# Sharing a PSUM tile between feature halves, and opening the second weight group early, at the joint between a transformer's output projection and its last MLP

## The chip, the core and the metric

The kernel runs on one core of a Trainium2 chip. TensorE (PE in the profile) multiplies matrices and writes into PSUM, VectorE (DVE) and ScalarE (ACT) do the elementwise work, GpSimd (POOL) does tiny per-row arithmetic here, and SyncE (SP) issues the DMA transfers. The metric is the time of one execution in microseconds (us), lower is better.

## The reference

The program is a two-layer backbone over 512 latent tokens and 256 context tokens of width 1024. Layer 0 mixes tokens by pooling, layer 1 by attention; each layer ends in an MLP of inner width 4096. Only the part around the end of layer 1 matters here:

```python
        y_lat, y_ctx = attention_mixer(h_lat, h_ctx, w_qkv[j], g_q[j], g_k[j], w_o[j], not last)
        x = x + gt1 * rms_norm(y_lat, g_mix_post[i])
        m_lat = sq_relu_mlp(modulate(rms_norm(x, g_mlp_pre[i]), sh2, sc2), w_mlp_in[i], w_mlp_out[i])
        x = x + gt2 * rms_norm(m_lat, g_mlp_post[i])

def sq_relu_mlp(h, w_in, w_out):
    return jnp.square(jax.nn.relu(h @ w_in)) @ w_out
```

In layer 1 only the 512 latent tokens go through the MLP. `attention_mixer` ends in a product with `w_o`, which this text calls the output stage.

## The kernel before

**Number format.** Each fp32 operand of a product is kept as two parts, hi and lo: ACT casts the value to the multiplier's format (hi) and DVE subtracts (lo = value - hi). One product is then three matmuls: hi with hi, hi with lo, lo with hi. "A product" below is one such matmul.

**The output stage** (`output`, lines 1334 to 1354). The 512 tokens are four tiles t = 0 to 3 of 128 rows. `attn_mm` (matmul line 1292) multiplies by the two column halves of `w_o`; `attn_ev` multiplies the result by the gate (DVE, line 326) and sums its squares (ACT, line 170); `rstd` turns the sum into a scale on POOL (lines 177 to 185). `norm_r` adds to the residual `xr` (DVE, line 329), `norm_s` sums the squares of the new `xr` (ACT line 170, then POOL), and `norm_c` scales the row (line 521 on ACT or 523 on DVE). When two tiles are ready, `norm_pair` calls `modulated_pair`: 16 TensorE transposes (line 350) turn the pair so that features lie on the partitions, DVE and ACT apply scale and shift (lines 358 and 361), and the result is written as hi (`h1H`, in `ra`) and lo (`h1L`, in `rb`). There are eight blocks k of 128 features. For the first pair (t = 0, 1) hi and lo are written four blocks at a time (lines 369 and 370), for the second pair (t = 2, 3) two at a time (lines 364 and 365, `fine`).

**The second MLP** (`mlp1`, from line 860). The inner width is cut in 16 groups of 256 features. A group's first half (`Inner.part`, matmul line 562) multiplies the tokens by 256 columns of `w_mlp_in`, as two feature halves f = 0 and 1 of 128 features each, over eight blocks k and three matmuls per block: 24 products for each f and each stretch of tokens. `relu` (line 573) and a square (line 902) on ACT follow. Groups go in pairs: the second half, with `w_mlp_out`, is done for two groups together by seven products of sums (`product`, matmul line 911) on operands X and W that `put` and `both` make on ACT and DVE (lines 883 and 889). A tile for a first half comes from the PSUM pool `psA`, which has two tiles of two banks. In group 0 each f has its own tile, and the tokens are cut in two chunks of 256, one in each bank: chunk 0 is the first pair, chunk 1 the second. Group 1 and all later ones do all 512 tokens in one matmul.

**What sets the order.** The steps of the output stage are put into a list with due times (`at(time, function, ...)`), which is sorted and traced. The framework then plans the order of each engine's instructions by its own model of time and puts in the waits; an instruction marked as kept in program order stays behind the one traced before it on its engine. In the first pass of `mlp1` (p = 0) the preparation of W is kept in this way. Weights arrive by a DMA into one of three `raw` buffers and are split into hi and lo (`split`, lines 142 and 145). The weights of group 0 are loaded and split within the output stage (due times 20 and 32); those of group 1 are loaded and split by `w_in(1, 1, ins[1], True)` at the start of `mlp1`, into `ra[:, 0:4096]`, which up to then holds the attention's output. Chunk 0 of group 0 is due at 41 and 42, the second pair at 47.4.

Of the kernel before, what the change touches and what calls it, by code (L numbers as in the profile page):

```python
# [68 lines left out]
def backbone(ctx: ExitStack, tc, x, ctx_in, w_ada, w_pool, pool_scale, w_qkv, g_q, g_k, w_o, w_mlp_in,  # L69
# [265 lines left out]
    def modulated_pair(t, i, s, hi, lo, works, wide, fine, on_act):  # L335
        place = lambda z, ks: z[:, ks, slice(t * P, (t + 2) * P)]
        ci = 0 if t < NL else 1
        sh = (SH1, SH2)[s] * KT
        pss = []
        for q in range(4):  # L340
            if not wide:
                ps = psB.tile([P, 2, 256], F32, tag="b", name="psx")
            elif q % 2 == 0:
                both = psA.tile([P, 4, 256], F32, tag="a", name="psx")
            if wide:
                ps = both[:, 2 * (q % 2):2 * (q % 2) + 2, :]
            for kk in range(2):
                k = 2 * q + kk
                for u in range(2):
                    te.transpose(ps[:, kk, u * P:(u + 1) * P], works[u][:, k * P:(k + 1) * P], ident)  # L350
            pss.append(ps)
        for q in range(4):
            h = works[q // 2][:, 512 * (q % 2):512 * (q % 2) + 512].rearrange("p (k n) -> p k n", n=256)
            for kk in range(2):
                k = 2 * q + kk
                sa, b = avec[i][s][:, k, ci:ci + 1], mods[i][:, sh + k, ci:ci + 1]
                if not on_act[k]:
                    ve.tensor_scalar(out=h[:, kk, :], in0=pss[q][:, kk, :], scalar1=sa, scalar2=b,
                                     op0=ALU.mult, op1=ALU.add)
                else:  # L360
                    sc.activation(h[:, kk, :], pss[q][:, kk, :], AF.Identity, scale=sa, bias=b)
            if fine:
                ks = slice(2 * q, 2 * q + 2)
                sc.copy(place(hi, ks), h)  # L364
                ve.tensor_tensor(out=place(lo, ks), in0=h, in1=place(hi, ks), op=ALU.subtract)  # L365
            elif q % 2:
                ks = slice(2 * q - 2, 2 * q + 2)
                h = works[q // 2].rearrange("p (k n) -> p k n", n=256)
                sc.copy(place(hi, ks), h)
                ve.tensor_tensor(out=place(lo, ks), in0=h, in1=place(hi, ks), op=ALU.subtract)  # L370

# [150 lines left out]
        else:  # L522
            ve.tensor_scalar(out=accv[:, t, :], in0=xr[:, t, :], scalar1=r, scalar2=None, op0=ALU.mult)

    def norm_pair(t, i, s, hi, lo, wide, fine, on_act):
        modulated_pair(t, i, s, hi, lo, [accv[:, t, :], accv[:, t + 1, :]], wide, fine, on_act)

    def chunks0(g):
        if g == 0:
# [1 line left out]
        return [[(0, 0, 0, 384), (1, 0, 384, 384)]], [(0, 2, 384, 0)]  # L531

    def chunks1(g):
        if g == 0:
            return [[(0, 0, 0, 256)], [(1, 0, 256, 256)]], [(0, 2, 256, 0)]
        return [[(0, 0, 0, 512)]], [(0, 1, 512, 0)]

    CHUNKS = {TOK: chunks0, LAT: chunks1}
    hids0 = [(rb[:, 3072 * b:3072 * b + 1536], rb[:, 3072 * b + 1536:3072 * b + 3072]) for b in range(2)]
    class Inner:  # L540
        def __init__(self, g, w, aH, aL, hid, chunks_of, ntok):
            self.w, self.a, self.ntok = w, (aH, aL), ntok
            self.hid = hid and [z.rearrange("p (f n) -> p f n", n=ntok) for z in hid]
            self.chunks, self.pieces = chunks_of(g)
            self.ps, self.opened = {}, set()

        def part(self, c, f, ks=range(KT)):
            (wH, wL), (aH, aL) = self.w, self.a
            if f not in self.ps:
                self.ps[f] = psA.tile([P, 2, 512], F32, tag="a", name="psin")  # L550
            ps, fs = self.ps[f], slice(f * P, (f + 1) * P)
            for k in ks:
                for n, (w, a) in enumerate(((wH, aH), (wH, aL), (wL, aH))):
                    for bank, o, t0, ln in self.chunks[c]:
# [7 lines left out]
                        te.matmul(ps[:, bank, o:o + ln], w[:, k, fs], rhs, start=start,  # L562
                                  stop=(k == KT - 1 and n == 2), skip_group_check=len(ks) < KT)

        def relu(self, f):
            r = work_tile()[:, 0:self.ntok]
# [149 lines left out]
    def w_in(i, g, rg, pin=False, wait=None):  # L716
        return rg.load(w_mlp_in[i, g], 256, pin, wait)
# [139 lines left out]
        before_last()  # L857
        finish(0, [part, (NG - 1, inner.hid, wo_)], order, last)

    def mlp1(inner, last):  # L860
        nonlocal xr, gate, junk
        for t in range(NL):
            sy.dma_start(spill[:, t], xr[:, t])
# [34 lines left out]

        def squares(inner, q):
            for f in range(2):  # L900
                inner.part(len(inner.chunks) - 1, f)
                sc.activation(F[:, q, f, :], inner.relu(f), AF.Square)
            return F[:, q, :, 0:256], F[:, q, :, 256:512]

# [397 lines left out]
        if ch:  # L1302
            rs[t] = rstd(ss1[t], 1 + len(ps1[t]))

    first1 = []

    def attention(st, base, unit_t):
        at = lambda i, fn, *args: st.at(base + unit_t * i, fn, *args)
# [23 lines left out]
        at(39.281, gate_diag if False else gate_rows, 1, GT1, 0)  # L1332

    def output(st, base):
        at = lambda i, fn, *args: st.at(base + i, fn, *args)
        for n, (ch, t) in enumerate(((0, 0), (0, 1), (1, 0), (0, 2), (1, 1), (0, 3), (1, 2), (1, 3))):
            b = 5.2 * n
            at(b, attn_mm, ch, t)
            at([5.2, 10.4, 15.6, 20.8, 26, 31.2, 36.4, 41.6][n], attn_ev, ch, t)
            if ch:  # L1340
                at([16.9, 27.3, 37.7, 42.9][t], norm_r, t, (False, False, False, False)[t])
                at([17.9, 28.3, 38.7, 43.9][t], norm_s, t, (False, False, False, False)[t])
                at([18.814, 29.214, 39.614, 46.4][t], norm_c, t, (False, True, True, False)[t])
                if t % 2:
                    at(36.3 if t == 1 else 47.4, norm_pair, t - 1, 1, 1, h1H, h1L, t == 1, t == 3,
                       ((False, True, True, False, True, False, True, False), (True, False, True, False, True, False, True, False))[t // 2])
# [22 lines left out]
    mlp1(first1[0], last1)  # L1369


_INS = ["x", "ctx", "w_ada", "w_pool", "pool_scale", "w_qkv", "g_q", "g_k", "w_o", "w_mlp_in", "w_mlp_out"]
# [79 lines left out]
```

## Time and profile before

| | us |
|---|---|
| median of three runs | 1178.41 (1176.73 to 1180.56) |
| the profiled execution | 1178.11 |
| its span, first to last instruction | 1176.3 |
| PE busy | 1145.3 (97%) |
| DVE busy | 938.4 (80%) |
| ACT busy | 635.0 (54%) |

All times of the trace below count from the start of the span. The output stage's matmuls run from 784.7 to 830.7; group 0's first product starts at 830.43 and group 1's last at 860.21. A row of the timeline gives the start, the length, the engine, the line, the operation, its output and inputs with shapes, and how many instructions are merged in it; in square brackets stand the idle time before it and what ended that. A row of the windows gives, after the stretch and its length, each engine's busy time and number of instructions, then the granted TensorE clock (1.00 is full), the share of the DMA engines and GB/s. Matmuls overlap, so the pace of a run of them is read from their starts.

### The profile page before, as it was taken

To read this page: it belongs to the slowest core of one execution; us is meant where nothing else is said; L and a number is where in the kernel's file an instruction comes from. 1 tells how busy PE (TensorE), PEld (TensorE's weight loads), DVE (VectorE), ACT (ScalarE), POOL (GpSimd) and SP (SyncE) were. 2 spreads that over 40 slices of the span, in tenths; PEclk is the share of its full clock that TensorE was granted. 3 is DMA by queue.
4 is the path that set the end of the run, shared out by engine and by line. 5 is a ranking of instruction groups with operands and counts; after the bars stand their busy time and mean duration, and the time that the engine had idled before them with its cause. 6 is when DMAs were issued, how large, how long until landed. Compare 5 with 4: busy or idle time off the path is not lost. (4 is left out here: it accounts for less than half of the span.)

```text
span 1176.3 us, 15958 instructions
## 1 busy us (share of the span) xinstructions
PE 1145.3 (97%) x6172; PEld 989.6 (84%) x6172; DVE 938.4 (80%) x1538; ACT 635.0 (54%) x1080; POOL 68.1 (6%) x120
## 2 busy tenths in 40 slices
PE   7889999999999999999999999999899999999997
PEld 5569898899899988998887889988888888888886
DVE  4677788889988998997778599877687779778876
ACT  4576655454454435555585378862676346435522
POOL 2030000000000000000231200001100000000001
PEclk9999999999999999999999999999999999999999
DMA  9983113343433434343422101115234123304212
GB/s 369 392 319 115 50 60 143 116 157 126 143 143 143 143 122 150 115 146 112 179 72 104 41 1 37 37 72 189 98 116 170 49 95 143 108 36 144 108 35 109
DMA packets 25516, 147.32 MB, mean 125 GB/s; under 512 B 2785, under 2 KB 5217, under 8 KB 9698
## 3 DMA queue, kind: packets, MB, share of 16 engines
q1 hardware_dynamic: 25442, 146.32, 34.1%
q8 instruction: 48, 0.79, 0.3%
q14 instruction: 26, 0.21, 0.1%
HBM read 138.96 MB, written 7.34 MB: 124 GB/s over the span
## 5 line engine op out<-in xcount | busy, mean ns | idle before, releaser
L807 PE MATMUL pso<-units,rb 128*128 128x512 f32 x1152 | 278.4, 392 | 0.0
L807 PEld LDWEIGHTS pso<-units,rb 128*128 128x128 f32 x1152 | 214.8, 188 | 41.2
L273 DVE SCALAR_TENSOR_TENSOR rows<-raw,cond,rows 128x256 f32<-128x256 f32 x280 | 127.0, 478 | 2.0
L819 DVE TENSOR_TENSOR acc<-acc,pso 128x512 f32<-128x512 f32 x129 | 85.4, 676 | 42.2 <-PE pso L807 42.1
L562 PE MATMUL psin<-ra,rb 128*128 128x512 f32 (+1 forms) x432 | 104.0, 343 | 1.6 <-ACT ra L364 1.6
L911 PE MATMUL pso<-units,pairs 128*128 128x512 f32 x336 | 82.3, 389 | 0.0
L562 PE MATMUL psin<-ra 128*128 128x512 f32 x256 | 80.6, 390 | 0.0
L562 PEld LDWEIGHTS psin<-ra,rb 128*128 128x128 f32 x432 | 70.9, 193 | 11.0 <-ACT ra L364 1.9
L911 PEld LDWEIGHTS pso<-units,pairs 128*128 128x128 f32 x336 | 63.1, 188 | 13.1
L915 DVE TENSOR_TENSOR acc<-acc,pso 128x512 f32<-128x512 f32 x72 | 48.7, 682 | 28.5 <-PE pso L911 28.5
L183 POOL TENSOR_SCALAR ms<-ss 128x1 f32<-128x1 f32 x20 | 11.2, 561 | 1006.7 <-ACT junk L170 963.8
L686 PE MATMUL psin<-ra,units 128*128 128x384 f32 x336 | 65.7, 337 | 0.4 <-ACT psin L698 0.4
L686 PE MATMUL psin<-sums,units 128*128 128x384 f32 x336 | 63.9, 337 | 0.0
L686 PEld LDWEIGHTS psin<-ra,units 128*128 128x128 f32 x336 | 59.7, 188 | 3.9 <-ACT psin L698 0.9
L686 PEld LDWEIGHTS psin<-sums,units 128*128 128x128 f32 x336 | 58.9, 188 | 1.7
L145 DVE TENSOR_TENSOR units<-raw,units 128x1024 fp32r<-128x1024 f32 (+2 forms) x49 | 55.3, 1150 | 3.6 <-ACT units L142 3.5
L562 PEld LDWEIGHTS psin<-ra 128*128 128x128 f32 x256 | 48.1, 188 | 10.0
L142 ACT CAST units<-raw 128x1024 fp32r<-128x1024 f32 (+2 forms) x49 | 46.8, 995 | 14.5 <-PE pso L807 10.4
L562 PE MATMUL psin<-rb 128*128 128x512 f32 (+1 forms) x144 | 53.4, 372 | 0.2 <-DVE rb L365 0.2
L817 ACT COPY acc<-pso 128x512 f32<-128x512 f32 x48 | 27.1, 587 | 49.0 <-PE pso L807 48.5
L1054 PE MATMUL psq<-units,ra 128*128 128x512 f32 x216 | 51.6, 392 | 0.0
L562 PE MATMUL psin<-rb,ra 128*128 128x512 f32 x128 | 49.8, 389 | 0.0
(277 smaller groups left out, 2347.2 us busy)
## 6 DMA issues: line engine op xcount, KB each, us to landing
raw<-in_w_ada SPq DMA_DIRECT2D x48, 1024.0 KB, 5.0
raw<-in_w_mlp_in SPq DMA_DIRECT2D x32, 1024.0 KB, 4.9
raw<-in_w_mlp_out SPq DMA_DIRECT2D x32, 1024.0 KB, 5.4
raw<-in_w_qkv SPq DMA_DIRECT2D x6, 1024.0 KB, 4.8
spill<-xr SPq DMA_DIRECT2D x10, 512.0 KB, 6.8
xr<-spill SPq DMA_DIRECT2D x10, 512.0 KB, 6.9
raw<-in_w_o SPq DMA_DIRECT2D x4, 1024.0 KB, 4.8
xr<-in_x SPq DMA_DIRECT2D x4, 512.0 KB, 6.3
```

What stands on the lines that cost most here:

```text
L142: a = sc.copy(hi, raw)
L145: b = ve.tensor_tensor(out=lo, in0=raw, in1=hi, op=ALU.subtract)
L183: gp.tensor_scalar(out=ms[:, 0:1], in0=ss[:, parts - 1:parts], scalar1=rest, scalar2=EPS, op0=ALU.add, op1=ALU.add)
L273: ve.scalar_tensor_tensor(out=r, in0=raw[:, k, :], scalar=cond[:, k, c:c + 1], in1=r, op0=ALU.mult, op1=ALU.add)
L562: te.matmul(ps[:, bank, o:o + ln], w[:, k, fs], rhs, start=start, stop=(k == KT - 1 and n == 2), skip_group_check=len(ks) < KT)
L686: te.matmul(bank, w[k], a[k], start=start and k == 0 and m == 0, stop=stop and k == 3 and m == 2, skip_group_check=True)
L807: te.matmul(pss[h][:, 0:cols[h][1]], a[:, f, ts_], w[:, f, cols[h][0]:sum(cols[h])], start=(n == 0 and not seeded[t]), stop=(n == len(seq) ...
L817: sc.copy(d, ps)
L819: ve.tensor_tensor(out=d, in0=d, in1=ps[:, 0:w], op=ALU.add)
L911: te.matmul(ps, a, w, start=(m == 0), stop=(m == len(seq) - 1))
L915: ve.tensor_tensor(out=M[n][:, t], in0=M[n][:, t], in1=ps, op=ALU.add)
L1054: te.matmul(ps, a[:, k, sl], w[:, k % 4, :], start=(k == 0 and n == 0), stop=(k == KT - 1 and n == 2))
```

## The change

Five things are changed, and nothing in the mathematics.

1. The first pair's second half of hi and lo (blocks 4 to 7) is no longer written where `modulated_pair` would do it. It is handed out (`late`) and written by a step `upper_half`, due at 41.65; its ACT copy is kept behind what was traced before it, which is the sum of squares of the last tile of the output stage.
2. Groups 0 and 1 become `paired`: both feature halves of a group use one `psA` tile, f = 0 in bank 0 and f = 1 in bank 1, and the two token chunks are the two halves of a bank.
3. Group 1 is also cut in two chunks of 256 tokens (four sets of 24 products of 256 columns in place of two sets of 24 of 512).
4. Group 1's weights are loaded at due time 26, and those of f = 0 are split in the output stage (`half_early`, due at 36) into `rb[:, 4096:6144]`. The other half is split at the start of `mlp1`.
5. Group 0's chunk 0 is traced as f = 0 and f = 1 over blocks 0 to 3, then over blocks 4 to 7. Between these come 12 products of group 1 (f = 0, chunk 0, blocks 0 to 3, due at 41.9); its other 12 (blocks 4 to 7) are due at 47.5, just after the second pair's transposes. `squares` then leaves out what has been done.

```diff
@@ modulated_pair
             elif q % 2:
                 ks = slice(2 * q - 2, 2 * q + 2)
                 h = works[q // 2].rearrange("p (k n) -> p k n", n=256)
+                if late is not None and q == 3:
+                    late.append((place(hi, ks), place(lo, ks), h))
+                    continue
                 sc.copy(place(hi, ks), h)
                 ve.tensor_tensor(out=place(lo, ks), in0=h, in1=place(hi, ks), op=ALU.subtract)
@@ chunks1
-        if g == 0:
-            return [[(0, 0, 0, 256)], [(1, 0, 256, 256)]], [(0, 2, 256, 0)]
+        if g < 2:
+            return [[(0, 0, 0, 256)], [(0, 256, 256, 256)]], [(0, 1, 512, 0)]
         return [[(0, 0, 0, 512)]], [(0, 1, 512, 0)]
@@ class Inner
-            if f not in self.ps:
+            if self.paired and not self.ps:
+                t = psA.tile([P, 2, 512], F32, tag="a", name="psin")
+                self.ps = {q: t[:, q:q + 1, :] for q in range(2)}
+            elif f not in self.ps:
                 self.ps[f] = psA.tile([P, 2, 512], F32, tag="a", name="psin")
+            if self.f0 and f == 0:
+                wH, wL = self.f0
...
+                            start = start and not (self.paired and (f, bank) in self.opened)
+                            self.opened.add((f, bank))
@@ mlp1
         def squares(inner, q):
             for f in range(2):
-                inner.part(len(inner.chunks) - 1, f)
+                for c in range(len(inner.chunks)):
+                    if (c, f) not in begun.get(inner, ()):
+                        inner.part(c, f)
                 sc.activation(F[:, q, f, :], inner.relu(f), AF.Square)
...
-        wi = [None, w_in(1, 1, ins[1], True)]
+        wi = [None, None]
+        hi, lo = (ra[:, z:z + 2048] for z in (0, 2048))
+        hi, lo = (z.rearrange("p (k n) -> p k n", n=256) for z in (hi, lo))
+        put((hi[:, :, P:], lo[:, :, P:]), raw1[0][:, :, P:], True)
+        second.w = hi, lo
+        begun = {inner: ((0, 0), (0, 1)), second: ((0, 0),)}
...
-            a12, a22 = squares(inner_of(2 * p + 1), 1)
+            a12, a22 = squares(inner_of(2 * p + 1) if p else second, 1)
@@ before attention and output
+    def half_early():
+        hi, lo = (rb[:, z:z + 1024].rearrange("p (k n) -> p k n", n=P) for z in (4096, 5120))
+        sc.copy(hi, raw1[0][:, :, 0:P])
+        ve.tensor_tensor(out=lo, in0=raw1[0][:, :, 0:P], in1=hi, op=ALU.subtract)
+        first1.append(Inner(1, (None, None), h1H, h1L, None, chunks1, LAT, True, (hi, lo)))
@@ output
+        def upper_half():
+            hi, lo, h = halves[0]
+            tc.keep_in_program_order(sc.copy(hi, h))
+            ve.tensor_tensor(out=lo, in0=h, in1=hi, op=ALU.subtract)
+
+        at(41.65, upper_half)
         for f in range(2):
-            at((41, 42)[f], lambda *a: first1[0].part(*a), 0, f)
+            for h in range(2):
+                at(41.7 + f / 10 + h, lambda *a: first1[0].part(*a), 0, f, range(4 * h, 4 * h + 4))
...
-        at(20, lambda: first1.append(Inner(0, w_in(1, 0, early, False, raws), h1H, h1L, None, chunks1, LAT)))
+        at(20, lambda: first1.append(Inner(0, w_in(1, 0, early, False, raws), h1H, h1L, None, chunks1, LAT, True)))
         at(32, lambda: split(*raws[0]))
+        at(26, lambda: raw1.append(raw_load(w_mlp_in[1, 1], rawp).rearrange("p (k n) -> p k n", n=256)))
+        at(36, half_early)
+        for h in range(2):
+            at((41.9, 47.5)[h], lambda ks: first1[1].part(0, 0, ks), range(4 * h, 4 * h + 4))
```

More of the change, by code (lines that the diff above doesn't have):

```diff
@@ L333, in scaled, with modulated_pair @@
         ve.tensor_scalar(out=dst, in0=xr[:, t, :], scalar1=r[:, 0:1], scalar2=None, op0=ALU.mult)
-    def modulated_pair(t, i, s, hi, lo, works, wide, fine, on_act):
+    def modulated_pair(t, i, s, hi, lo, works, wide, fine, on_act, late=None):
         place = lambda z, ks: z[:, ks, slice(t * P, (t + 2) * P)]
@@ L523, in norm_c, with norm_pair @@
             ve.tensor_scalar(out=accv[:, t, :], in0=xr[:, t, :], scalar1=r, scalar2=None, op0=ALU.mult)
-    def norm_pair(t, i, s, hi, lo, wide, fine, on_act):
-        modulated_pair(t, i, s, hi, lo, [accv[:, t, :], accv[:, t + 1, :]], wide, fine, on_act)
+    def norm_pair(t, i, s, hi, lo, wide, fine, on_act, late=None):
+        modulated_pair(t, i, s, hi, lo, [accv[:, t, :], accv[:, t + 1, :]], wide, fine, on_act, late)
     def chunks0(g):
@@ L540, in backbone, with __init__ @@
     class Inner:
-        def __init__(self, g, w, aH, aL, hid, chunks_of, ntok):
-            self.w, self.a, self.ntok = w, (aH, aL), ntok
+        def __init__(self, g, w, aH, aL, hid, chunks_of, ntok, paired=False, f0=None):
+            self.w, self.a, self.ntok, self.paired, self.f0 = w, (aH, aL), ntok, paired, f0
             self.hid = hid and [z.rearrange("p (f n) -> p f n", n=ntok) for z in hid]
@@ L561, in part @@
                             rhs = a[:, k, t0:t0 + ln]
+                            start = start and not (self.paired and (f, bank) in self.opened)
+                            self.opened.add((f, bank))
                         te.matmul(ps[:, bank, o:o + ln], w[:, k, fs], rhs, start=start,
-                                  stop=(k == KT - 1 and n == 2), skip_group_check=len(ks) < KT)
+                                  stop=(k == KT - 1 and n == 2), skip_group_check=len(ks) < KT or self.paired)
         def relu(self, f):
@@ L858, in mlp0, with mlp1 @@
         finish(0, [part, (NG - 1, inner.hid, wo_)], order, last)
-    def mlp1(inner, last):
+    def mlp1(inner, second, last):
         nonlocal xr, gate, junk
@@ L1334, in output @@
     def output(st, base):
[L1335 removed]
+        at, halves = lambda i, fn, *args: st.at(base + i, fn, *args), []
         for n, (ch, t) in enumerate(((0, 0), (0, 1), (1, 0), (0, 2), (1, 1), (0, 3), (1, 2), (1, 3))):
@@ L1368, in backbone @@
     mlp0(first[0], hids0, (4, 5, 0, 1, 2, 3), extra0, mid0, last0, before0)
-    mlp1(first1[0], last1)
+    mlp1(*first1, last1)
 _INS = ["x", "ctx", "w_ada", "w_pool", "pool_scale", "w_qkv", "g_q", "g_k", "w_o", "w_mlp_in", "w_mlp_out"]
```

4 lines of the change are left out of this document (2 added, 2 removed).

## The prediction

> **What bounds the kernel now.** I read the page first, then one window from the joint to almost the last matmul, then the joint itself.
>
> ```profile
> span 1176.3 us, 15958 instructions
> PE 1145.3 (97%) x6172; PEld 989.6 (84%) x6172; DVE 938.4 (80%) x1538; ACT 635.0 (54%) x1080; POOL 68.1 (6%) x120
> 848.00:1168.00 320.00, 320.00 (x1431) 265.14 (x1431) 252.22 (x296) 156.72 (x207) 2.66 (x6) 1.00 0.28 102
> ```
>
> From 848 to 1168 PE is busy in every microsecond at full clock. So whatever moves PE earlier at the joint moves the end by as much, unless a new wait takes it back. The joint, in four stretches: group 0's first token chunk, the gap, its second chunk, group 1.
>
> ```profile
> 830.43:836.65 6.22, 6.22 (x54) 6.18 (x52) 3.29 (x4) 3.06 (x6) 1.49 (x3) 1.00 0.09 33
> 836.65:841.57 4.92, 1.69 (x14) 1.29 (x13) 2.73 (x6) 2.58 (x6) 0.79 (x2) 1.00 0.18 70
> 841.57:849.40 7.83, 7.61 (x48) 7.35 (x48) 6.97 (x8) 4.87 (x7) 0.00 (x0) 0.78 0.11 33
> 849.40:860.43 11.03, 11.03 (x50) 9.12 (x49) 9.05 (x10) 7.80 (x10) 0.00 (x0) 1.00 0.39 144
> ...
> 843.60:846.80 3.20, 3.20 (x18) 3.20 (x16) 0.50 0.00 0
> ```
>
> PE loses time in two ways: it is idle in most of the 4.92 us of the gap, and right after it the clock is granted at 0.50 for 3.2 us. The idle pieces and their releasers, from the timeline of PE, with four rows for the pace:
>
> ```profile
> 836.53 0.28 PE L562 MATMUL psin<-ra,rb 128*128 128x256 f32 x1
> 838.41 1.53 PE L350 MATMUL psx<-ident,acc 128*128 128x128 f32 x12 [1.59 <-DVE acc L523]
> 841.57 0.50 PE L562 MATMUL psin<-ra,rb 128*128 128x256 f32 x2 [1.64 <-ACT ra L364]
> 842.30 0.39 PE L562 MATMUL psin<-rb 128*128 128x256 f32 x1 [0.23 <-DVE rb L365]
> ...
> 843.60 0.63 PE L562 MATMUL psin<-ra,rb 128*128 128x256 f32 x2
> 846.80 0.48 PE L562 MATMUL psin<-ra,rb 128*128 128x256 f32 x2
> 847.12 0.28 PE L562 MATMUL psin<-rb 128*128 128x256 f32 x1
> 849.27 0.28 PE L562 MATMUL psin<-ra,rb 128*128 128x256 f32 x1
> ```
>
> From 847.12 to 849.27 lie 18 products of 256 columns: 0.119 us each. Group 1's 48 of 512 columns take 11.03 us, 0.230 each. What sets the 838.41 is the chain of waits (start, length, what), with ACT's and DVE's own rows around its beginning:
>
> ```profile
> 831.26 0.61 issue
> 831.87 0.48 ACT junk L170 x2
> 832.52 0.89 POOL ms L183
> 833.48 0.56 POOL rs L185
> 834.04 2.61 issue
> 837.56 317.36 issue
> ...
> 830.80 0.41 DVE L326 TENSOR_TENSOR acc<-psy,gate 128x256 f32<-128x256 f32 x1
> 830.93 1.04 ACT L369 CAST ra<-acc 128x1024 fp32r<-128x1024 f32 x1
> 832.00 1.23 DVE L370 TENSOR_TENSOR rb<-acc,ra 128x1024 fp32r<-128x1024 f32 x1 [0.79 <-ACT ra L369]
> 834.07 1.28 DVE L329 SCALAR_TENSOR_TENSOR xr<-acc,rs,xr 128x1024 f32<-128x1024 f32 x1 [0.85 <-POOL rs L185]
> ```
>
> It is the last tile's normalization, queued behind the upper-half cast at 830.93. From 837.56 on the chain has only "issue": PE runs on.
>
> **The change part by part.**
>
> *Group 1's 24 products in the gap.* Twelve take 12 x 0.119 = 1.43 us. The first twelve follow group 0's blocks 0 to 3, the second stand behind the transposes, against idle pieces of 1.59 and 1.64 us: both fit and delay nothing. After the gap group 1 has 72 products of 256 columns: 72 x 0.119 = 8.57 us in place of 11.03. **Gain 2.46 us.** (All 96 would take 11.42: the narrower cut costs 0.4 us, in these figures.)
>
> *The clock.* From 843.60 to 846.80, the stretch at 0.50, 15 products take 3.20 us, 0.213 each; at 0.119 they would take 1.79. With both idle pieces down to some 0.2 us I expect no drop: **gain 1.4 us**. Bounds: 0, the drop stays; 1.5, a little beyond the 3.2 us.
>
> *The upper half written later.* The sum of squares at 831.87 comes up to 0.62 us earlier, as the 1.04 us cast no longer stands before it (DVE has read that tile at 830.80 + 0.41 = 831.2). The cast then ends near 832.8 and the subtraction (1.23) near 834.1. If DVE does it before the residual, as listed, the residual starts at 834.1, as now (834.07): 0. If the residual goes first, it can start at 832.9, since POOL's 0.89 also shrinks: up to 1.1 earlier, of which PE, now busy to 836.65 + 1.43 = 838.1, can use some 0.4. If both end late, 0.6 is lost. I take 0, the listed order. Group 0's blocks 4 to 7 need this subtraction: PE reaches them at 830.43 + 36 x 0.12 = 834.8, covered by the 12 products of group 1; without them PE would wait 0.8 us.
>
> *The early split and its load.* Rows for its cost and cover:
>
> ```profile
> 804.13 0.33 SPq L123 DMA_DIRECT2D raw<-in_w_mlp_in  x1
> 823.15 0.69 DVE L326 TENSOR_TENSOR acc<-psy,gate 128x512 f32<-128x512 f32 x1 [4.09 <-PE psy L1292]
> 823.94 0.60 ACT L170 ACTIVATE junk<-psy 128x512 bf16<-128x512 f32 x1 [3.36 <-DVE acc L326]
> 844.77 1.05 ACT L883 CAST ra<-raw 128x1024 fp32r<-128x1024 f32 x1
> 847.12 1.22 DVE L883 TENSOR_TENSOR ra<-raw,ra 128x1024 fp32r<-128x1024 f32 x1
> ```
>
> The one DMA is issued at 804.13 already now, so on SP's queue nothing is passed that matters, and the buffer is held until after the joint as before: 0. The half split costs ACT 1.05 and DVE 1.22 us; ACT idles 3.36 and DVE 4.09 us right where it is due: 0. If that cover is missed, it stands before the first pair's work and PE starts late by up to 2.3 us, the other bound. The same work disappears behind the joint, where DVE is nearly full. POOL issues nothing new.
>
> *Later stages.* PE comes 3.9 us sooner, DVE and ACT only 2 to 3. One idle piece of DVE, and the two closest meetings:
>
> ```profile
> 851.20 0.69 DVE L889 TENSOR_TENSOR work<-hid 128x512 f32<-128x512 f32 x1 [1.72 <-ACT hid L902]
> 870.61 0.68 DVE L883 TENSOR_TENSOR pairs<-hid,pairs 128x512 fp32r<-128x512 f32 x1
> 874.03 1.98 PE L911 MATMUL pso<-units,pairs 128*128 128x512 f32 x8
> 877.72 2.29 DVE L145 TENSOR_TENSOR ra<-raw,ra 128x2048 fp32r<-128x2048 f32 x1 [2.29 <-ACT ra L142]
> 882.19 0.39 PE L562 MATMUL psin<-ra 128*128 128x512 f32 x1
> ```
>
> The third product's operand is ready 2.7 us before its use, group 3's weights 2.2 us. With DVE ahead by half a split (1.07) and by the idle time it now spends waiting for group 0 (1.7), both hold by about 1 us. I take 0; at worst 2 us come back.
>
> **Sum:** 2.46 + 1.4 + 0 = 3.9 us. The profiled execution took 1178.1 us, 0.3 below the median; 1178.1 - 3.9 = 1174.2.
>
> **The rivals.**
>
> *Clock stays halved* (idle near 838 and the transposes are enough): gain 2.5, 1175.6. For it: the drop came 2 us after PE had resumed, so it looks back over several microseconds. Against: the gap loses 2.9 of 3.2 idle us.
>
> *The gain is taken back* by the late operands above: 2 us, 1176.2.
>
> *The shared tile makes TensorE wait for ScalarE: slower.* Today each f has its own tile. If waits are kept by whole PSUM tile, the matmuls of f = 1 must wait until `relu` of f = 0 has read. Rows that bear on this:
>
> ```profile
> 553.53 2.35 PE L686 MATMUL psin<-ra,units 128*128 128x384 f32 x12 [0.43 <-ACT psin L698]
> 59.65 3.13 PE L490 MATMUL pspool<-rb,ra 128*128 128x256 f32 x24
> 62.90 0.60 ACT L170 ACTIVATE junk<-pspool 128x512 bf16<-128x512 f32 x1 [2.32 <-PE pspool L490]
> 862.48 0.61 ACT L573 ACTIVATE work<-psin 128x512 f32<-128x512 f32 x1
> ```
>
> At 553.53 product 3 of layer 0's MLP writes bank 1 of a tile and waits for a copy that touches only bank 0 of it; at 62.90 ACT, idle, reads a first bank only when the 24 matmuls of both are done. So such waits are likely. They are harmless while ACT is prompt: group 1's f = 0 covers the `relu` of group 0, and group 0's f = 1 (24 x 0.119 = 2.9 us) that of group 1. But now ACT reads group 1's f = 0 at 862.48, when its products ended near 849.40 + 24 x 0.230 = 854.9: 7.6 us late, its queue standing behind the W chain. Were it as late now, PE would idle 7.6 + 0.6 - 2.9 = 5.3 us and lose 1.4 to the clock: -3.9 + 6.7 = +2.8, or 1180.9; with a second such wait for group 0, beyond 1182. It decides from 6.8 us of lateness on. Against it: the planner knows the wait and can put that `relu` first, and before 849 ACT is not behind.
>
> [...] The row at 553.53 shows a wait across banks, so here the measurement decides for the wait.
>
> **How the numbers follow.** A measurement of this kernel can tell about 0.3%, 3.5 us, from no change. Against the profiled 1178.1 that bound lies at 1174.6. Forecast, 1174.2, its own range 1172.8 to 1175.1 (the chain's bounds of 0.4 earlier and 0.6 later, the clock's, and a short wait in the later stages): 0.62, of which 0.08 falls above 1174.6. Clock or late operands, 1175.6 to 1176.2: 0.16. Shared-tile wait, 1178 to 1184: 0.22, nearly all of it beyond 0.3%, since such a stall brings its own clock drop and may come twice; 0.03 within. So faster 0.54, same 0.08 + 0.16 + 0.03 = 0.27, slower 0.19. The range runs from 1172.3 to 1180.5 and leaves out the worse half of the last rival.
>
> **What would show it.** Right: 24 products of line 562 with 256 columns in the gap, twelve on each side of the transposes; idle pieces below 0.5 us; granted clock 1.00 from 840 to 850; group 1 done near 856.4; 320 us later no PE idle. Wrong: PE idle released by ACT line 573 between 845 and 865 (shared tile), PE idle released by line 883 or 145 between 868 and 880 (late operands), a clock of 0.50 after the gap, or the first pair's hi and lo later than 830.4.

## The result and the profile after

The changed kernel is slower. Its median is 1188.39 us (five runs, 1184.1 to 1190.34) against 1178.41 (five runs): a ratio of 1.0074 (95% interval 1.0058 to 1.009). Timed once more in a later experiment it took 1184.32 against 1178.45: 1.0048 (1.003 to 1.0066). The forecast was 1174.2.

The profiled execution took 1188.43 us. The head of its page:

```profile
span 1186.6 us, 16056 instructions
PE 1151.7 (97%) x6220; PEld 995.5 (84%) x6220; DVE 938.1 (79%) x1539; ACT 635.4 (54%) x1081; POOL 67.0 (6%) x120
```

PE is busy 6.4 us longer with 48 more instructions, the second token chunk of group 1. The span is 10.3 us longer. To see where, I cut it at group 0's first product and at the last matmul row. The timeline of PE after, with all idle pieces of the joint (groups 0 and 1 are cut in chunks of 256 tokens, group 2 in one of 512, so a row of 512 columns is group 2's or a later one's; the rows of 851.07 and 852.27 have no idle time before them and are explained below):

```profile
833.85 0.28 PE L572 MATMUL psin<-ra,rb 128*128 128x256 f32 x1
842.95 1.47 PE L350 MATMUL psx<-ident,acc 128*128 128x128 f32 x12
846.06 0.50 PE L572 MATMUL psin<-ra,rb 128*128 128x256 f32 x2 [1.40 <-ACT ra L364]
846.79 0.39 PE L572 MATMUL psin<-rb 128*128 128x256 f32 x1 [0.23 <-DVE rb L365]
851.07 0.52 PE L572 MATMUL psin<-ra,rb 128*128 128x256 f32 x3
852.27 0.28 PE L572 MATMUL psin<-ra,rb 128*128 128x256 f32 x1
854.62 0.39 PE L572 MATMUL psin<-ra,rb 128*128 128x256 f32 x1 [2.06 <-ACT work L583]
861.61 0.50 PE L572 MATMUL psin<-ra,rb 128*128 128x512 f32 x1 [2.37 <-ACT work L583]
862.93 2.08 PE L923 MATMUL pso<-ra,pairs 128*128 128x512 f32 x4 [0.50 <-ACT pairs L893]
892.25 0.50 PE L572 MATMUL psin<-ra 128*128 128x512 f32 x1 [0.60 <-ACT ra L142]
1178.90 0.88 PE L817 MATMUL pso<-units 128*128 128x256 f32 x6
```

and the last row of the same timeline before:

```profile
1168.58 0.88 PE L807 MATMUL pso<-units 128*128 128x256 f32 x6
```

From the first product to that last row lie 345.05 us after (833.85 to 1178.90) and 338.15 before (830.43 to 1168.58). I call this length the stretch below. So 6.9 us come from the joint on and 3.4 us from ahead of it. Those 3.4 us are complete by 94 us, where the instructions of the two kernels and their order are the same; what they are stands in the last section.

The idle pieces tell the story. The piece of 1.59 us is gone, as forecast, and the one of 1.64 is 1.40. But two new ones are ended by ACT's line 583, the `relu` that reads the PSUM tile (line 573 before): 2.06 and 2.37 us. All pieces add up to 7.16 us after and 3.46 before. The two other new ones are short waits for late operands (0.50 at 862.93, 0.60 at 892.25). The windows of PE after, from the joint on:

```profile
833.85:842.95 9.10, 9.10 (x76) 8.95 (x75) 4.13 (x6) 3.35 (x6) 1.88 (x5) 1.00 0.15 59
855.30:858.70 3.40, 3.40 (x18) 3.40 (x17) 0.21 (x1) 0.00 (x0) 0.00 (x0) 0.50 0.00 0
861.90:865.40 3.50, 3.00 (x8) 2.02 (x8) 3.42 (x5) 1.56 (x3) 0.00 (x0) 0.53 0.22 54
900.00:1178.00 278.00, 278.00 (x1239) 230.10 (x1238) 220.93 (x264) 128.29 (x168) 2.67 (x6) 1.00 0.27 97
```

The clock is not halved behind the gap now (granted 1.00 from 843 to 855), but it is halved once behind each of the two waits for a `relu`; from 900 on PE is busy in every microsecond. ACT's own timeline shows why it was late, first after, then around the same place before:

```profile
852.08 1.04 ACT L893 CAST ra<-work 128x1024 fp32r<-128x1024 f32 x1 [2.61 <-DVE work L899]
853.03 1.04 ACT L893 CAST units<-raw 128x1024 fp32r<-128x1024 f32 x1
853.98 0.59 ACT L583 ACTIVATE work<-psin 128x512 f32<-128x512 f32 x1
859.16 1.90 ACT L142 CAST rb<-raw 128x2048 fp32r<-128x2048 f32 x1 [3.94 <-PE psin L572]
860.97 0.59 ACT L583 ACTIVATE work<-psin 128x512 f32<-128x512 f32 x1
868.93 0.60 ACT L583 ACTIVATE work<-psin 128x512 f32<-128x512 f32 x1
879.81 0.60 ACT L583 ACTIVATE work<-psin 128x512 f32<-128x512 f32 x1 [6.28 <-PE psin L572]
```

```profile
848.75 0.60 ACT L573 ACTIVATE work<-psin 128x512 f32<-128x512 f32 x1 [2.93 <-PE psin L562]
851.72 1.04 ACT L883 CAST ra<-work 128x1024 fp32r<-128x1024 f32 x1
```

*The first wait.* In the order that the framework planned for PE, 14 products of group 1's f = 0 stand among the 24 of group 0's f = 0. So the last of the 24 is one of the three at 851.07, and PE's signal to ACT stands in the trace at 851.37. ACT does not take the `relu` then. Two casts of the W chain come before it in ACT's order, and the first of them waits for DVE until 852.08 (ACT is idle for 2.61 us, 0.7 of it after 851.37). The `relu` runs at 853.98, 2.6 us late. PE has only 10 products of group 1 left to do meanwhile, up to 852.27, and then waits before f = 1 of group 0, which is in the same tile. In the kernel before, the `relu` (848.75) stands ahead of the same casts (851.72 is the first).

*The second wait* is at group 2's first product. The two `psA` tiles are handed out in turn, so group 2 gets group 0's, which is free only after the `relu` of f = 1 at 860.97. Before that `relu` ACT does the 1.90 us split of group 2's weights. The split goes into the place of group 0's weights, so it too can start only when PE is done with group 0 (the row of 859.16 ends an idle time of 3.94 with PE). PE has nothing else to do: group 1's f = 1 shares a tile with its f = 0, which ACT reads only at 868.93, and it stands behind group 2's f = 0 in PE's order.

### The profile page after: what moved, and what is told of

Same layout as the page of the kernel before. It is cut to its first block, busy times and chain, and to the rows that moved or that the text cites. A ratio compares the mean times of both kernels' runs of the same rounds, so it can differ in the third digit from the quotient of the medians.

```text
span 1186.6 us, 16056 instructions
## 1 busy us (share of the span) xinstructions
PE 1151.7 (97%) x6220; PEld 995.5 (84%) x6220; DVE 938.1 (79%) x1539; ACT 635.4 (54%) x1081; POOL 67.0 (6%) x120
## 5 line engine op out<-in xcount | busy, mean ns | idle before, releaser
L572 PE MATMUL psin<-ra,rb 128*128 128x256 f32 (+1 forms) x464 | 111.7, 342 | 5.8 <-ACT work L583 4.4
L572 PEld LDWEIGHTS psin<-ra,rb 128*128 128x128 f32 x464 | 77.0, 196 | 15.9 <-ACT work L583 5.1
L572 PE MATMUL psin<-ra 128*128 128x512 f32 (+1 forms) x256 | 76.4, 376 | 0.6 <-ACT ra L142 0.6
L572 PE MATMUL psin<-rb 128*128 128x512 f32 (+1 forms) x160 | 58.1, 364 | 0.2 <-DVE rb L365 0.2
L572 PE MATMUL psin<-rb,ra 128*128 128x512 f32 (+1 forms) x128 | 48.1, 376 | 0.0
```

## The experiments

The theory was: PE waits for the `relu`s because waits are kept by whole PSUM tile and ACT's order puts the `relu` late. The rivals: the tile alone is harmless and the early products, their place, or the late upper half cost the time; or the clock does. Since one profile can hold a halving of the clock and another of the same kernel not, each stretch stands with the number of halvings in it. "Medians" are this kernel's and that of the kernel before in the same comparison.

| kernel | medians, us | ratio (95%) | stretch | halvings in the joint |
|---|---|---|---|---|
| before | 1178.41 | | 338.15 | 1 |
| after | 1188.39 / 1178.41 | 1.0074 (1.0058 to 1.009) | 345.05 | 2 |
| after, again | 1184.32 / 1178.45 | 1.0048 (1.003 to 1.0066) | 344.42 | 2 |
| relu_last | 1178.91 / 1178.29 | 1.0008 (0.9996 to 1.0019) | 335.43 | 0 |
| relu_last, again | 1177.07 / 1178.45 | 0.9988 (0.9977 to 0.9999) | 336.82 | 1 |
| twelve_pinned | 1182.51 / 1178.29 | 1.0041 (1.0027 to 1.0056) | 339.15 | 1 |
| relu_last_pinned | 1175.68 / 1178.2 | 0.9977 (0.9964 to 0.9991) | 334.29 | 0 |
| shared_only | 1180.09 / 1178.29 | 1.0016 (1.0002 to 1.003) | 339.41 | 0 |
| shared_only_relu_last | 1179.09 / 1178.29 | 1.0006 (0.9993 to 1.002) | 337.29 | 0 |
| own_tiles | 1175.26 / 1178.2 | 0.9978 (0.9964 to 0.9992) | 333.83 | 0 |
| own_no_late | 1174.71 / 1178.45 | 0.9971 (0.9959 to 0.9982) | 334.14 | 0 |
| late_only | 1177.87 / 1178.2 | 0.9997 (0.9985 to 1.001) | 336.35 | 0 |
| before_tail | 1178.88 / 1178.2 | 1.0007 (0.9996 to 1.0018) | 336.65 | 0 |

**The `relu`s of a paired group moved behind the products of both halves** (relu_last).

```diff
             for f in range(2):
                 for c in range(len(inner.chunks)):
                     if (c, f) not in begun.get(inner, ()):
                         inner.part(c, f)
-                sc.activation(F[:, q, f, :], inner.relu(f), AF.Square)
+                if not inner.paired:
+                    sc.activation(F[:, q, f, :], inner.relu(f), AF.Square)
+            if inner.paired:
+                for f in range(2):
+                    sc.activation(F[:, q, f, :], inner.relu(f), AF.Square)
```

> The changed kernel, with one edit: in a paired group the ReLU and square of f = 0 and f = 1 both come after the products of both halves, so no product is behind a read of its tile; same tiles, same early products, same result. Theory A (the shared PSUM tile makes TensorE wait for ScalarE's ReLU): the idle pieces of 2.06 and 2.37 us released by that ReLU go, the second drop of the clock with them, and group 1 runs right behind group 0; from group 0's first product to group 1's last some 26.5 to 28 us where before took 30.0, so 1174.5 to 1177. Rival B (the early products ahead of the transposes, and ScalarE's and VectorE's queues as rearranged, are the loss, the ReLU wait only shows it): TensorE waits as long elsewhere, for W or X operands, and the time stays above 1183.

No PE row of the joint is ended by line 583 any more; what is left is the gap's 1.40 and 0.23. The stretch falls by 9.6 us against the changed kernel, some 2.9 of them, by an estimate, its two halvings (1.39 to 1.50 us each between kernels of the same joint, below). The ratio to the kernel before is 1.0008, so nearly the whole loss is given back, though the expected gain on the kernel before (1174.5 to 1177) did not come. ACT is no faster here:

```profile
857.34 1.90 ACT L142 CAST rb<-raw 128x2048 fp32r<-128x2048 f32 x1 [0.81 <-DMA raw<-in_w_mlp_in]
859.15 1.08 ACT L583 ACTIVATE work<-psin 128x512 f32<-128x512 f32 x2
```

Both `relu`s of group 0 still stand behind the casts and the split. But no product of group 0 is behind its own tile's read any more, and the rest of group 1's products lie between group 0's last product and group 2's first.

**The second twelve products kept behind the transposes** (twelve_pinned). In the changed kernel 70 of the 72 products of the gap stand ahead of the twelve transposes on PE, ten of them from the twelve that are due after.

```diff
+        def second_part(ks, pin):
+            ordered[0] = pin
+            first1[1].part(0, 0, ks)
+            ordered[0] = False
         for h in range(2):
-            at((41.9, 47.5)[h], lambda ks: first1[1].part(0, 0, ks), range(4 * h, 4 * h + 4))
+            at((41.9, 47.5)[h], second_part, range(4 * h, 4 * h + 4), h == 1)
```

> The changed kernel, with one edit: the second twelve early products of group 1 are kept in program order, behind the second pair's transposes, as their due time says; in the changed kernel 10 of these 12 stand ahead of 12 transposes. Theory A: the transposes come some 1.2 us sooner and the 1.40 us idle piece before group 0's second chunk is filled, but the ReLU waits are as long or longer, so little is won: 1185 to 1188. Rival B: the loss falls by more than half, below 1183.

The transposes and two idle pieces of this kernel's PE, then four rows of its ACT:

```profile
838.19 1.47 PE L350 MATMUL psx<-ident,acc 128*128 128x128 f32 x12
841.30 0.50 PE L572 MATMUL psin<-ra,rb 128*128 128x256 f32 x2 [0.21 <-ACT ra L364]
853.15 0.50 PE L572 MATMUL psin<-ra,rb 128*128 128x512 f32 x1 [2.37 <-ACT work L583]
...
847.00 0.60 ACT L583 ACTIVATE work<-psin 128x512 f32<-128x512 f32 x1 [2.30 <-PE psin L572]
848.16 1.03 ACT L893 CAST ra<-work 128x1024 fp32r<-128x1024 f32 x1
850.70 1.90 ACT L142 CAST rb<-raw 128x2048 fp32r<-128x2048 f32 x1 [0.55 <-PE psin L572]
852.50 0.59 ACT L583 ACTIVATE work<-psin 128x512 f32<-128x512 f32 x1
```

The transposes start 8.01 us after the first product (830.18), where the changed kernel has 9.10, and the piece behind them falls from 1.40 to 0.21. The first wait for the `relu` is gone, which was not expected: the planner now has that `relu` (847.00) ahead of the W cast (848.16), and ACT reads as soon as PE is done. The tile is shared as before, and PE has only 7 products of group 1 to do meanwhile; so it is ACT's order that made the first wait long. The wait of 2.37 for group 0's tile is untouched: the split (850.70) still stands before the `relu` of f = 1 (852.50). The time, 1182.51, is just below the 1183 that was set for the rival; theory A's 1185 to 1188 counted on both waits. The kernel stays slower than the one before. Its profiled execution (1178.87) was well below its median, so the ratio is what counts here.

**Both edits together** (relu_last_pinned; the two diffs above).

> The changed kernel with both edits: both ReLUs of a paired group behind both halves, and the second twelve early products kept behind the second pair's transposes. From group 0's first product to the start of the last matmul, before took 338.2 us and the run with the ReLU edit alone 335.4. If the two faults (ReLU wait, twelve products ahead of the transposes) are separate, the 1.40 us piece goes to about 0.2 and this stretch is 334.0 to 334.8, with no wait for the ReLU. Rival: the planner or a late operand takes it back, and the stretch stays at 335.4 or more. The whole time less than before by 2 to 4 us only if the part ahead of the joint is as in before; if the clock's drops at the start are again more than in before, the whole gains nothing.

The ends of the stretch, the transposes and all idle pieces of the joint:

```profile
830.44 0.28 PE L572 MATMUL psin<-ra,rb 128*128 128x256 f32 x1
838.45 1.47 PE L350 MATMUL psx<-ident,acc 128*128 128x128 f32 x12
841.56 0.50 PE L572 MATMUL psin<-ra,rb 128*128 128x256 f32 x2 [0.21 <-ACT ra L364]
842.29 0.38 PE L572 MATMUL psin<-rb 128*128 128x256 f32 x1 [0.23 <-DVE rb L365]
1164.73 0.88 PE L817 MATMUL pso<-units 128*128 128x256 f32 x6
```

Of 7.16 us of idle time 0.44 are left, and the kernel is faster than the one before: 0.9977, or 2.5 us.

**The shared tile alone** (shared_only: the changed kernel without the early load, split and products and without the late upper half; groups 0 and 1 paired, group 1 in two chunks; group 0's chunk 0 traced as before).

```diff
-        at(26, lambda: raw1.append(raw_load(...)))
-        at(36, half_early)
-        for h in range(2):
-            at((41.9, 47.5)[h], lambda ks: first1[1].part(0, 0, ks), range(4 * h, 4 * h + 4))
...
-        wi = [None, None]
...
+        wi = [None, w_in(1, 1, ins[1], True)]
+        second = Inner(1, wi[1], h1H, h1L, None, chunks1, LAT, True)
+        begun = {inner: ((0, 0), (0, 1))}
```

> The kernel before, with only the shared tile and the narrower cut of groups 0 and 1: no early split, no early products, no late upper half; ReLU of f = 0 ahead of f = 1's products as in the changed kernel. Theory A: TensorE waits for the ReLU here as well, at least 2 us, and the time is above before, 1181 to 1188. Rival B: only the narrower cut costs, 0.4 us: 1178 to 1179.

Its PE timeline has two waits for a `relu`, the first before group 0's f = 1, the second before group 2's f = 1:

```profile
846.16 0.39 PE L572 MATMUL psin<-ra,rb 128*128 128x256 f32 x1 [0.82 <-ACT work L583]
872.22 0.50 PE L572 MATMUL psin<-ra,rb 128*128 128x512 f32 x1 [0.75 <-ACT work L583]
```

So sharing has its price by itself, 1.57 us of waits and a ratio of 1.0016. That is less than theory A's 2 us and 1181, and more than the narrower cut alone: the stretch is 2.8 us above that of before_tail below, both without a halving. Group 2's f = 0 takes group 0's tile here too, ahead of group 1's f = 1, but without a wait: the two `relu`s of group 0 run at 845.50 and 849.33, right behind their products. In the changed kernel they run at 853.98 and 860.97. So the 4.43 us there come from sharing together with an ACT order that puts the reads late.

**The same with the `relu`s last** (shared_only_relu_last; shared_only with the edit of relu_last).

> The same with both ReLUs behind both halves. Theory A: no idle piece released by the ReLU; the narrower cut alone is left: 0 to 1 us above before, and the gap and the clock drop of before are back. Rival B: the same as the run without this edit, within 1 us.

The stretch falls from 339.41 to 337.29, by 2.1 us, and no PE row waits for a `relu`. The medians, 1179.09 against 1180.09, lie too close to tell the two theories apart, and the ratio of 1.0006 can't be told from 1. Most of the gap is back (0.66 and 1.64 us), the halving behind it is not.

**The early products with tiles of their own** (own_tiles: group 0 unpaired with its two `psA` tiles as before; group 1's f = 0 in a one-bank tile of another pool, f = 1 in a `psA` tile with 512-column products; the second twelve pinned; the `relu` between the halves, as in the changed kernel).

```diff
-            if self.paired and not self.ps:
-                t = psA.tile([P, 2, 512], F32, tag="a", name="psin")
-                self.ps = {q: t[:, q:q + 1, :] for q in range(2)}
+            if self.paired and f == 0 and f not in self.ps:
+                self.ps[f] = psB.tile([P, 512], F32, tag="b", name="psin0").unsqueeze(1)
             elif f not in self.ps:
                 self.ps[f] = psA.tile([P, 2, 512], F32, tag="a", name="psin")
```

> The early products without a shared tile: group 0 has one tile for each feature half as in before, group 1's f = 0 has a single bank of the other PSUM pool, its f = 1 a tile of its own and all 512 tokens in one matmul; the second twelve early products are kept behind the transposes; early split and late upper half as in the changed kernel; ReLUs in the order of before. Theory A (whole-tile waits): no wait for the ReLU although the ReLU stands between the halves as in the changed kernel; the stretch from group 0's first product to the last matmul's start is 334 to 336. Rival B (the early products or the early split are the loss): above 338.

PE's timeline, where the only idle piece of the joint stands among the transposes:

```profile
844.52 1.14 PE L350 MATMUL psx<-ident,acc 128*128 128x128 f32 x9
846.25 0.66 PE L350 MATMUL psx<-ident,acc 128*128 128x128 f32 x4 [0.58 <-DVE acc L358]
```

No PE row of the joint waits for a `relu`. The program has them between the halves as in the changed kernel, but the planned order differs: both `relu`s of group 0 (853.90 and 856.95) stand ahead of the split (857.44), and the first also ahead of the W casts (855.07). So this run shows that early products go well with tiles of their own; by itself it does not separate the tile from ACT's order. Relu_last and twelve_pinned do: the one takes the wait away with ACT as late as ever, the other with the tile shared as ever. The ratio is 0.9978.

**The same without the late upper half** (own_no_late: own_tiles with `late` and `upper_half` taken out).

> The kernel with own tiles for the feature halves, with the upper half written where before writes it. If the late upper half is what lets the last tile's normalization come sooner: the transposes come 0.8 to 1.1 us later after group 0's first product than the 7.9 us with it, and the stretch to the last matmul's start is 0.5 to 1 us above 333.8. If not: the same stretch within 0.3 us.

The stretch is 334.14 instead of 333.83, 0.3 us longer, where 0.5 to 1 was expected if the late half mattered; the transposes start 8.16 us after the first product instead of 7.90, with a wait of 0.40 us ahead of them. The ratio, 0.9971 (0.9959 to 0.9982), is the best of all kernels here, though the intervals of this one, own_tiles and relu_last_pinned overlap. The late upper half is worth nothing that was measured.

**The late upper half alone** (late_only: the kernel before with `late`, `upper_half` and group 0's chunk 0 by halves of k).

> The kernel before with only the upper half of the first pair written later, and group 0's first chunk traced by halves of k; own tiles, no early products, no early split. If the chain of the last tile's normalization gains by it: the residual and the transposes come 0.9 to 1.1 us sooner after group 0's first product than the 7.98 us of before, and TensorE waits 0.5 to 0.8 us for the upper half's subtraction, which nothing covers here; in all 0 to 0.9 us gained in the stretch. If the subtraction goes first: nothing.

PE now waits for the half that is written late:

```profile
839.13 0.39 PE L572 MATMUL psin<-rb 128*128 128x256 f32 x1 [1.24 <-DVE rb L1370]
841.87 1.47 PE L350 MATMUL psx<-ident,acc 128*128 128x128 f32 x12
```

The transposes start 7.73 us after the first product (834.14) where the kernel before has 7.98: the chain gains 0.25 us, not the 0.9 to 1.1 expected, and PE's wait of 1.24 us is longer than the 0.5 to 0.8 expected. The time stays (0.9997).

**The kernel before with its last half-row of output written twice** (before_tail). It was to show whether the length of an execution shifts the clock of the next one.

```diff
             sy.dma_start(out[0, t * P:(t + 1) * P, n0:n1], xr[:, t, n0:n1])
+        if t == NL - 1:
+            sy.dma_start(out[0, t * P:(t + 1) * P, 512:D], xr[:, t, 512:D])
```

> The kernel before, with the last half row of the output written once more at the very end, behind its first writing: the same work up to the last output, some 2 us added at the end. Open is why the changed kernels lose more of the TensorE clock in the first 90 us, where every engine's instructions and waits are the same as in before. [...]

On that it decides nothing: the ratio of 1.0007 (0.9996 to 1.0018) fits the expected 2 us more as well as none. But its joint is instruction for instruction that of the kernel before, and its windows there are the best witness on the clock:

```profile
838.27:843.19 4.92, 1.69 (x15) 1.30 (x13) 2.74 (x6) 2.58 (x6) 0.79 (x2) 1.00 0.18 70
845.20:848.60 3.40, 3.40 (x31) 3.40 (x30) 2.54 (x2) 2.24 (x2) 0.00 (x0) 1.00 0.00 0
```

The gap is the same 4.92 us with 1.69 busy, and yet no halving follows. Its stretch is 336.65 us, 1.50 less than the kernel before with one.

**The changed kernel and relu_last once more** (after_again, relu_last_again; no edit). In their first profiles the part ahead of the joint took longer than in the kernel before.

> The changed kernel once more, unedited, timed beside before in the same call. In its first profile 6.9 us of the difference lay behind group 0's first product and 3.4 us ahead of it, where instructions and waits are those of before. If the part ahead is the luck of a few runs, the time is now 5 to 8 us above before and the stretch behind the first product again 345 us; if it belongs to this kernel, 8 to 10 us.

> The changed kernel with the ReLU edit alone, once more. The stretch behind the first product took 335.4 us, 2.7 less than in before, but ten runs were no faster than before, with a mean granted clock of 0.9925 against 0.9955. If that was chance, the time is now 1 to 3 us below before; if it is this kernel's own, again within 1 us of before and again with the lower clock.

Both came out as expected if that part is chance: the changed kernel 5.9 us above the kernel before with a stretch of 344.42, relu_last 1.4 below. The changed kernel, its timeline of PE:

```profile
851.36 0.39 PE L572 MATMUL psin<-ra,rb 128*128 128x256 f32 x1 [0.56 <-ACT work L583]
856.86 0.50 PE L572 MATMUL psin<-ra,rb 128*128 128x512 f32 x1 [2.37 <-ACT work L583]
888.39 0.50 PE L572 MATMUL psin<-ra 128*128 128x512 f32 x1 [1.08 <-ACT ra L142]
```

Here the clock was halved behind the gap (granted 0.50 from 845.1 to 848.1), which slowed PE's products while ACT's order stayed, so PE waited only 0.56 us for the first `relu`, not 2.06; the second wait is the same 2.37. A slower PE hides part of the wait, so clock and waits don't add. Relu_last keeps its gap of 1.40 and 0.23 us in both profiles. The first, then the second, by the windows behind it:

```profile
848.52:865.00 16.48, 16.25 (x127) 15.79 (x128) 13.94 (x16) 10.84 (x15) 0.00 (x0) 1.00 0.32 111
```

```profile
844.60:847.90 3.30, 3.30 (x17) 3.30 (x17) 3.29 (x5) 1.81 (x2) 0.00 (x0) 0.50 0.22 27
```

The same instructions with the same idle time: one has a halving, the other has none, and their stretches differ by 1.39 us.

## Why the prediction was wrong

**The step that failed** is the one that set the third rival aside, so that the wait for the shared tile entered the sum as nothing: "They are harmless while ACT is prompt: group 1's f = 0 covers the `relu` of group 0", and "the planner knows the wait and can put that `relu` first, and before 849 ACT is not behind." ACT indeed was not behind; it sat idle from 849.47. But the planner put the `relu` behind two W casts, the first of which waited for DVE. And the cover was not 24 products (2.9 us) but 10, as the other 14 had been planned in between. The rival's own sum then fits: 2.6 us of lateness, plus 0.6 for the `relu`, less 1.2 of cover, is 2.0; 2.06 were measured. That sum had been filled in for group 1, from the row of 862.48, and not for group 0, where the kernel before has the `relu` ahead of those casts. Relu_last (no product behind the read) and twelve_pinned (the read ahead of the casts) each take this wait away, and so does own_tiles.

**The second wait was foreseen only as "a second such wait".** That group 2 needs group 0's tile, that a split of 1.90 us can stand before the read that frees it, and that nothing is left to cover it once group 1's f = 1 waits for its own `relu`, is in no step of the prediction. This wait is 2.37 us in the changed kernel, in its second profile and in twelve_pinned, whatever the first one does: split and `relu` both become possible when group 0's last product ends.

**The wait across banks** was rightly taken from the measurement: the row of 553.53 has one of 0.43 us, and the 2.06 us at 854.62 are one more. The waits here are those of the program's own tracking, which goes by tile. In own_tiles, without a shared tile, no PE row of the joint waits for a `relu`.

**The 24 products in the gap: size right, place wrong.** The second twelve were taken to stand behind the transposes, where they were due; ten of them were planned ahead. The transposes came 1.1 us later than in twelve_pinned and 1.40 us of the second piece stayed. Relu_last_pinned has them where the prediction had them, and its pieces are the 0.2 us that it named. Against before_tail, both without a halving, its stretch is 2.36 us shorter; own_tiles has 2.82 and own_no_late 2.51. The forecast term was 2.46, and the measured medians of the three are 2.5, 2.9 and 3.7 us below the kernel before's.

**The clock term of 1.4 us was right in size and wrong in whom it belongs to.** A halving costs 1.4 to 1.5 us (1.39 between the two profiles of relu_last, 1.50 between the kernel before and before_tail). But the gap of the kernel before is followed by one in the profiled execution and by none in before_tail, and relu_last, with a smaller gap, has it both ways. The changed kernel has none behind its gap in one profile and one in the other. The forecast counted as earned what was the luck of one profile. That the drop "looks back over several microseconds" was the author's guess from one drop 2 us behind PE's restart (841.57 to 843.55); no run shows what sets a drop off. The sum of 3.9 does come out between two single profiles (338.15 less 334.29); in the medians 2.5 of it is there.

**The upper half written later:** taken as 0, between 0.4 earlier and 0.6 later. Late_only has the chain 0.25 us sooner and own_tiles against own_no_late 0.26 sooner; neither changes the measured time. Without the early products to cover it the wait for this half is 1.24 us in late_only, where the prediction said 0.8. **The early split:** taken as 0, and nothing speaks against it: PE's first product was not late through it in relu_last_pinned (830.44). **The later stages:** taken as 0. In the changed kernel they gave two short waits, 0.50 at 862.93 for a product's operand and 0.60 at 892.25 for group 3's weights, which the prediction had named as a close meeting; in relu_last_pinned PE is busy throughout 870 to 1160.

**Two of the prediction's figures do not follow from its own terms.** With the clock's 1.4 the shared tile takes the whole gain back from 4.8 us of lateness on (4.8 + 0.6 - 2.9 + 1.4 = 3.9), not from 6.8. And the low end of its own range, 1172.8, lies below what the named bounds allow (1174.2 less 0.4 and 0.1 is 1173.7). Neither decides the outcome.

**What isn't settled.** Of the 6.9 us in the stretch, 3.7 are idle time, about 1.5 the second halving and 0.4 the narrower products. Another 0.6 are idle time that the pieces do not count, since a matmul's row (0.28 us) reaches beyond the start of the next (0.12 us on): from 852.27 to 854.62 PE loses 2.2 us against its usual 0.12 between starts, not 2.06. Some 0.7 us are not attributed to any row. Why the planner put the `relu` behind the casts in the changed kernel and ahead of them in twelve_pinned stays open. Nor was it tried whether the tracking of waits could be made finer than a tile.

## What to carry to other kernels

Before two accumulations share a PSUM tile, write down for each who reads it, where that read stands in its engine's order and what is in front of it: in this kernel a wait is kept for the whole tile, so a late read of one half holds both. Then ask which tile the next user will get, what stands before the read that frees it, and which products are left to cover that read: here the count in the program (24) was not the count in the planned order (10). And before a halved clock is entered in a sum as a cost that an edit removes, look at a second execution of the same kernel: if it comes and goes there, it is no property of the gap.

## What the runs showed of the hardware

Seven halvings stand in the joint, in the profiles of five runs, and each lasts 3.41 us at a granted clock of 0.50 (843.55 to 846.96 in the kernel before), behind idle pieces of 1.40 and 0.23 us as behind one of 2.37. Whether one comes behind the same idle time differs between executions: in relu_last's second profile the 1.40 and 0.23 us around twelve transposes were followed by a halving, in its first they were not. What sets it off no run here shows.

Ahead of the joint, too, the clock differs between executions. Two stretches near the start, before the change and after, by the windows (the clock is the third number from the right):

```profile
39.00:47.00 8.00, 6.56 (x62) 4.74 (x59) 4.87 (x11) 3.10 (x7) 0.00 (x0) 1.00 0.82 314
78.00:88.00 10.00, 8.65 (x80) 7.02 (x81) 7.55 (x15) 7.60 (x14) 1.95 (x4) 0.83 1.02 410
```

```profile
39.00:47.00 8.00, 6.86 (x44) 5.75 (x48) 3.67 (x9) 2.94 (x6) 0.00 (x0) 0.57 0.68 283
78.00:88.00 10.00, 7.43 (x57) 5.18 (x50) 8.47 (x17) 9.17 (x18) 3.23 (x7) 0.66 0.98 371
```

The instructions are the same, the granted clock is not; the second profile of the changed kernel shows 1.00 and 0.83 there, as the kernel before. Over eight profiles the start of group 0's first product follows the time at half clock in the first 95 us: 830.4 to 830.8 with 3.4 us of it (before, after_again, relu_last_again, own_no_late), 832.1 with 6.8 (before_tail), 833.9 and 834.1 with 13.7 (after, late_only), 836.6 with 17.1 (own_tiles). The kernel before and the changed one each stand in the first group in one profile, and before_tail, whose instructions up to there are those of the kernel before, in the second. So the 3.4 us ahead of the joint are put down to the clock. The spread of the kernel before goes with it: of 35 runs in one comparison, those with a mean granted clock of 0.997 took 1176.6 to 1177.8 us, those with 0.996 1178.0 to 1179.3, and those with 0.993 1180.0 to 1181.2 (two more lie at 0.992 and 0.998). What sets the clock at the start of an execution stays open.
